# A two-block transformer kernel: in the experts, all low parts of the weights on VectorE, and the products that read them last in each piece

## The chip, the cores and the metric

The kernel runs on one core of one Trainium2 chip. The metric is the device time of one execution in microseconds (us). The time before is the median of three runs. One more execution was taken by the hardware profiler, and every row below is from that one.

Names of engines, as the profile has them: PE is TensorE (its matmuls), PEld is TensorE's loading of the stationary operand, DVE is VectorE, ACT is ScalarE, POOL is GpSimd, SP is SyncE, which here only issues DMAs.

## The reference, cut to what matters

The whole program is a first block (modulation, a mixer of attention and an mLSTM, then a mixture of experts) and a second block of two layers. The change is in the experts of the first block. Sixteen experts each choose 128 of 1024 tokens; a chosen token goes through two 1024x1024 products, a gate, and a third 1024x1024 product, and the result is added back to its row:

```python
def ec_moe(x, w_router, w_e_gate, w_e_up, w_e_down):
    ...
    g, idx = lax.top_k(aff.transpose(0, 2, 1), cap)
    xs = jax.vmap(lambda xb, ib: xb[ib])(x, idx)
    a = jnp.einsum('becd,edf->becf', xs, w_e_gate)
    u = jnp.einsum('becd,edf->becf', xs, w_e_up)
    y = jnp.einsum('becf,efd->becd', jax.nn.silu(a) * u, w_e_down) * g[..., None].astype(x.dtype)
```

All is float32. The three weights of an expert are 4 MB each.

## The kernel before

**A product in pieces.** `product(xT, w3)` multiplies 128 tokens by a 1024x1024 weight. It takes the weight in 8 pieces of 128 rows (`k`), and a DMA brings two pieces at a time (`ewr`, 10 buffers, or `ahead`, 2 buffers). The float32 operands are split into a high part (rounded to the matmul's type float32r) and a low part, the difference. For a piece, ScalarE makes the high part `ewH` of the raw weight (line 1183), and then the low part `ewL` is raw minus high: for six of the eight pieces on VectorE (line 1187), for the fourth and the eighth on GpSimd (line 1185). `ewH` and `ewL` have four buffers each, so the parts of a piece can be made once the matmuls of the piece four back have read theirs.

**Six matmuls a piece.** The tokens, turned, are split in the same way (`xTH`, `xTL`, or `eTH`, `eTL` for the third product). For each half of 512 columns `mm3` issues three matmuls, high times high (line 145), high tokens times low weights (line 146) and low tokens times high weights (line 147). So the second matmul of a piece already needs `ewL`.

**An expert.** In the order of the code: the products up(e), gate(e+1) and down(e), 24 pieces. Around them stand the smaller steps. `slots` makes eight tiles `hot` on VectorE (line 1198, 16 buffers), multiplies them on TensorE (line 1199) and copies the result to `idxT` and `gsl` on VectorE. `tokens` gathers the chosen rows `xs` by a DMA that GpSimd issues (line 1208). `transposed` turns 128x128 blocks on TensorE (line 1162) and splits them with ScalarE and VectorE (lines 141 and 142). VectorE multiplies up by the activated gate into `ea` (line 1232), and after down it scales the result into `ey` (line 1238), which GpSimd adds to the rows in memory by an indirect DMA (`acc_scr`, line 1239; called the scatter below).

**What sets the order.** Each engine works through its own queue in order. The queues' order is made when the kernel is built: a scheduler places each instruction by a simulated timeline. SP's queue holds the weight DMAs; each waits until both low parts of the pair that had its buffer have been made. `issue_after` and the number of buffers set what can run ahead.

Of the kernel before, what the change touches and what calls it, by code (L numbers as in the profile page):

```python
# [14 lines left out]
AF = mybir.ActivationFunctionType  # L15
OP = mybir.AluOpType
# [106 lines left out]
def build(ctx, tc, A, out):  # L123
# [6 lines left out]
    V, S, G, PE, SY = nc.vector, nc.scalar, nc.gpsimd, nc.tensor, nc.sync  # L130
# [4 lines left out]
    def load(pool, src, shape, name, eng=None, dt=F32, **kw):  # L135
        t = pool.tile(shape, dt, name=name, **kw)
        (eng or SY).dma_start(t, src)
        return t

    def split(H, L, src):  # L140
        S.activation(H, src, AF.Copy)  # L141
        V.tensor_sub(L, src, H)  # L142

    def mm3(o, lh, rh, start, stop):
        PE.matmul(o, lh[0], rh[0], start=start, stop=False)  # L145
        PE.matmul(o, lh[0], rh[1], start=False, stop=False)  # L146
        PE.matmul(o, lh[1], rh[0], start=False, stop=stop)  # L147
# [266 lines left out]
    with ExitStack() as es:  # L414
# [62 lines left out]
        for f2 in range(4):  # L477
            wt = wstream(wp, win, 704 + 256 * f2)
            for f in (2 * f2, 2 * f2 + 1):
# [5 lines left out]
                for t0, n in ((0, 256), (256, 512), (768, 512)):  # L485
                    more(late, 1)
                    pa = ps.tile([P, 512], F32, name="acc", bufs=4)
# [304 lines left out]
    with ExitStack() as es:  # L792
# [7 lines left out]
        op = att.enter_context(tile_pool(name="o", bufs=8, side="right", reuse_waits="tile"))  # L800
# [117 lines left out]
        for job in [(h, g, []) for h in range(8) for g in range(4)] + [None]:  # L918
            w = weights(*job) if job else iter(())
# [43 lines left out]
    with ExitStack() as es:  # L963
# [6 lines left out]
        with ExitStack() as es2:  # L970
# [6 lines left out]
            for k in range(8):  # L977
                t = load(sp, h_scr[k, :, C:N], [P, T], "hr")
                H = hp.tile([P, T], F32R, name=f"hH{k}")
                L = hp.tile([P, T], F32R, name=f"hL{k}")  # L980
                split(H, L, t)
                h.append((H, L))
            for f in range(8):
                rf = load(sp, r_scr[f], [P, T], "hr")
                sg = []
                for n0 in (Z0, GL0, GA0):
                    more(late, 1)
                    w = wstream(wp, win, n0 + P * f, P, bufs=(2, 4))
                    t = sp.tile([P, T], F32, name="sg", bufs=3)
                    for t0 in (0, 512):  # L990
                        sl = slice(t0, t0 + 512)
                        more(late, 1)
                        pa = ps.tile([P, 512], F32, name="acc", tag="acc", bufs=4)
# [58 lines left out]
        for i in range(8):  # L1052
# [3 lines left out]
            pa = outs[i] if i in outs else out_product((i,))[0]  # L1056
            for n in range(2):
                ns = slice(512 * n, 512 * n + 512)
# [45 lines left out]
    with ExitStack() as es:  # L1104
# [12 lines left out]
        pa = ps.tile([P, P], F32, name="pa")  # L1117
# [31 lines left out]
    with ExitStack() as es:  # L1149
        wp = es.enter_context(tile_pool(name="ew", bufs=1, reuse_waits="tile"))  # L1150
        tp = es.enter_context(tile_pool(name="et", bufs=2, side="right", reuse_waits="tile"))
        sp = es.enter_context(tile_pool(name="ex", bufs=2, reuse_waits="tile"))
        ps = es.enter_context(tile_pool(name="ps6", bufs=1, space=PSUM))
        g2B = load(sp, mod_scr[0, 3072:4096].partition_broadcast(P), [P, D], "g2B", bufs=1)

        def transposed(src, nm):
            H = tp.tile([P, 8, P], F32R, name=nm + "H")
            L = tp.tile([P, 8, P], F32R, name=nm + "L")
            for hb in range(2):
                pt = ps.tile([P, 512], F32, name="tp", tag="tp", bufs=2)  # L1160
                for j in range(4):
                    PE.transpose(pt[:, j * P:(j + 1) * P], src[:, (4 * hb + j) * P:(4 * hb + j + 1) * P], ident)
                hs_ = slice(4 * hb, 4 * hb + 4)
                split(H[:, hs_].rearrange("p a b -> p (a b)"), L[:, hs_].rearrange("p a b -> p (a b)"), pt)
            return H, L

        loads = [0]

        def product(xT, w3):
            pa = ps.tile([P, 2, 512], F32, name="acc", tag="acc", bufs=3)  # L1170
            for k2 in range(4):
                if ew_ahead:
                    raw = ew_ahead.pop(0)
                elif loads[0] % NB < AH:
                    raw = ahead(w3, k2)
                else:
                    raw = load(wp, pairs(w3, k2), [P, 2, D], "ewr", bufs=NB - AH)
                loads[0] += 1
                for kk in range(2):
                    k = 2 * k2 + kk  # L1180
                    H = wp.tile([P, D], F32R, name="ewH", bufs=4)
                    L = wp.tile([P, D], F32R, name="ewL", bufs=4)
                    S.activation(H, raw[:, kk], AF.Copy)  # L1183
                    if k % 4 == 3:
                        G.tensor_tensor(L, raw[:, kk], H, op=OP.subtract)  # L1185
                    else:
                        V.tensor_sub(L, raw[:, kk], H)  # L1187
                    for n in range(2):
                        ns = slice(512 * n, 512 * n + 512)
                        mm3(pa[:, n], (xT[0][:, k], xT[1][:, k]), (H[:, ns], L[:, ns]), k == 0, k == 7)  # L1190
            return pa.rearrange("p a b -> p (a b)")

        def slots(e):

            pi = ps.tile([P, 512], F32, name="tp", tag="tp", bufs=2)
            for i in range(8):
                hot = sp.tile([P, P], F32, name="hot", bufs=16)
                V.tensor_scalar(hot, ktop[:, P:2 * P], codeT[:, 16 * i + e:16 * i + e + 1], None, op0=OP.is_equal)
                PE.matmul(pi[:, 0:2], hot, pick[:, i, e, :], start=i == 0, stop=i == 7)
            ins = V.tensor_copy(idxT[:, e:e + 1], pi[:, 0:1])  # L1200
            V.tensor_copy(gsl[:, e:e + 1], pi[:, 1:2])
            return ins

        at = lambda e: bass.IndirectOffsetOnAxis(ap=idxT[:, e:e + 1], axis=0)

        def tokens(e):
            xs = sp.tile([P, D], F32, name="xs")
            G.indirect_dma_start(out=xs, out_offset=None, in_=h2_scr, in_offset=at(e))
            return xs

        def gated(xT, e):
            a = sp.tile([P, D], F32, name="ea")
            S.activation(a, product(xT, A["w_e_gate"][0, e]), AF.Silu)
            return a


        chosen = slots(0)
        xs = tokens(0)
        slots(1)
        xT = transposed(xs, "xT")  # L1220
        xs = tokens(1)
        with tc.issue_after(chosen.ins):
            a = gated(xT, 0)
        for e in range(16):
            more_ = e + 1 < 16
            if more_:
                xTn = transposed(xs, "xT")
            if e + 2 < 16:
                slots(e + 2)
                xs = tokens(e + 2)  # L1230
            pu = product(xT, A["w_e_up"][0, e])
            V.tensor_tensor(a, pu, a, op=OP.mult)
            if more_:
                an = gated(xTn, e + 1)
            hT = transposed(a, "eT")
            pd = product(hT, A["w_e_down"][0, e])
            y = sp.tile([P, D], F32, name="ey")
            V.scalar_tensor_tensor(y, pd, gsl[:, e:e + 1], g2B, op0=OP.mult, op1=OP.mult)
            G.indirect_dma_start(out=acc_scr, out_offset=at(e), in_=y, in_offset=None, compute_op=OP.add)
            if more_:  # L1240
                xT, a = xTn, an
# [495 lines left out]
```

## Time and profile before

| | us |
|---|---|
| three runs: median (lowest to highest) | 3382.16 (3378.16 to 3387.02) |
| the profiled execution: its own time | 3381.72 |
| span of its instructions in the profile | 3379.5 |
| first product of the experts starts, about | 1510 |
| scatter of expert 0, of expert 15 | 1567.4, 2148.5 |

The span is 2.2 us shorter than the execution's own time, and this does not change with what runs inside. The experts' products and their scatters lie between 1510 and 2148 us of the span. A row of the timeline gives the start, the duration, the engine, the line, the operation, the tiles, how many equal instructions are merged in the row, and in brackets how long the engine had been idle and what ended it. A matmul's duration is longer than the distance to the next one, because matmuls overlap; the distance between starts is its cost.

### The profile page before, as it was taken

The numbers are of one execution on the slowest core, as the hardware profiler recorded it, in microseconds if no ns is written. First come the engines' busy times: TensorE is split into PE (matmuls) and PEld (weight loads), VectorE is DVE, ScalarE is ACT, GpSimd is POOL, SyncE is SP. The second block draws the span as 40 slices with busy tenths as digits, with TensorE's granted clock in tenths as the row PEclk, the third lists the DMA queues.
The fourth block names the chain that finished last, engine by engine and source line by source line (L and its number), as shares of the span: only waits on it lengthen the run. The fifth ranks groups of instructions, "written<-read, shape, count | busy, mean of one in ns | idle before, by whom it ended". The sixth has DMA issues, their size and how long they took to land.

```text
span 3379.5 us, 48130 instructions
## 1 busy us (share of the span) xinstructions
PE 3158.9 (93%) x17297; PEld 2648.0 (78%) x17297; DVE 2259.6 (67%) x4772; ACT 1550.5 (46%) x3076; POOL 900.5 (27%) x936
## 2 busy tenths in 40 slices
PE   7997998999999999959999998799999898999999
PEld 5885877999998887848887777598876777887787
DVE  4485778667767563589999888777626745642773
ACT  4223453655555222217777666531126724312780
POOL 0012232222221000525555444320013601101450
PEclk9998999999999999969999999899999999999999
DMA  8531011000004341459999988433210033111002
GB/s 294 144 120 35 36 42 64 5 17 8 8 10 149 117 122 59 172 208 346 362 373 365 331 313 295 136 93 115 73 41 32 1 127 122 51 50 49 32 26 100
DMA packets 224011, 425.95 MB, mean 126 GB/s; under 512 B 28684, under 2 KB 121468, under 8 KB 223772
## 3 DMA queue, kind: packets, MB, share of 16 engines
q1 hardware_dynamic: 215708, 393.51, 33.3%
q0 software_dynamic: 8064, 29.36, 3.0%
q8 instruction: 136, 2.23, 0.3%
q14 instruction: 103, 0.84, 0.1%
HBM read 379.22 MB, written 43.61 MB: 125 GB/s over the span
## 4 chain that ended last, share of the span: by engine, by line
PE 67%; DVE 12%; issue 6%; DMA 4%; POOL 4%; ACT 4%; SPq 0%; ACTq 0%; POOLq 0%; DVEq 0%
PE acc L146 13%; PE acc L145 13%; PE acc L147 13%; DVE ewL L1187 2%; POOL ewL L1185 2%; PE s L145 2%; PE s L147 2%; PE s L146 2%; PE t L904 2%; PE o L1606 1%; PE u L763 1%; PE s L1564 1%; PE ni L744 1%; PE t L1590 1%; PE o L146 1%
## 5 line engine op out<-in xcount | busy, mean ns | idle before, releaser
L145 PE MATMUL acc<-hH,wHL 128*128 128x512 f32 (+1 forms) x1296 | 485.2, 376 | 4.7 <-ACT wHL L141 4.1
L146 PE MATMUL acc<-hL,wHL 128*128 128x512 f32 (+1 forms) x1296 | 484.3, 374 | 0.8 <-DVE hL L142 0.8
L147 PE MATMUL acc<-hH,wHL 128*128 128x512 f32 (+1 forms) x1296 | 482.5, 373 | 0.0
L1187 DVE TENSOR_TENSOR ewL<-ewr,ewH 128x1024 fp32r<-128x1024 f32 x240 | 388.7, 1658 | 54.4 <-ACT ewH L1183 54.1
L1183 ACT ACTIVATE ewH<-ewr 128x1024 fp32r<-128x1024 f32 x320 | 336.4, 1060 | 148.6 <-PE acc L147 143.8
L145 PEld LDWEIGHTS acc<-hH,wHL 128*128 128x128 f32 x1296 | 244.5, 189 | 52.7 <-ACT wHL L141 6.7
L146 PEld LDWEIGHTS acc<-hL,wHL 128*128 128x128 f32 x1296 | 244.6, 189 | 45.8 <-issue 2.6
L147 PEld LDWEIGHTS acc<-hH,wHL 128*128 128x128 f32 x1296 | 244.2, 189 | 44.2 <-issue 1.6
L1185 POOL TENSOR_TENSOR ewL<-ewr,ewH 128x1024 fp32r<-128x1024 f32 x80 | 219.0, 2738 | 198.9 <-ACT ewH L1183 198.7
L142 DVE TENSOR_TENSOR wHL<-wr,wHL 128x512 fp32r<-128x512 f32 (+1 forms) x160 | 111.7, 702 | 224.0 <-ACT wHL L141 223.4
L146 PE MATMUL acc<-ewL,xTH 128*128 128x512 f32 x512 | 208.6, 407 | 23.2 <-POOL ewL L1185 15.6
L142 DVE TENSOR_TENSOR et<-t,et 128x512 fp32r<-128x512 f32 x264 | 179.6, 685 | 64.0 <-ACT et L141 62.3
L141 ACT ACTIVATE et<-t 128x512 fp32r<-128x512 f32 x264 | 156.4, 605 | 134.0 <-PE t L904 111.8
L141 ACT ACTIVATE wHL<-wr 128x512 fp32r<-128x512 f32 (+1 forms) x160 | 101.9, 639 | 247.2 <-PE acc L146 222.1
L147 PE MATMUL acc<-ewH,xTL 128*128 128x512 f32 x512 | 203.4, 397 | 2.9 <-DVE xTL L142 2.9
L183 POOL TENSOR_SCALAR E<-E,sm 128x512 f32<-128x512 f32 (+1 forms) x192 | 117.5, 630 | 327.0 <-ACT E L172 107.0
L145 PE MATMUL acc<-ewH,xTH 128*128 128x512 f32 x512 | 203.2, 401 | 0.8 <-ACT xTH L141 0.8
L302 DVE SCALAR_TENSOR_TENSOR ga<-gw,lh,ga 128x512 f32<-128x512 f32 x224 | 161.0, 747 | 52.1 <-DMA gw<-in_w_mod_dram 51.0
L329 POOL TENSOR_TENSOR ga<-ga,gw 1x128 f32<-1x128 f32 (+1 forms) x48 | 42.4, 884 | 427.0 <-ACT ga L315 411.9
L170 DVE TENSOR_REDUCE sm<-s 128x1 f32<-128x512 f32 (+1 forms) x192 | 113.2, 597 | 60.2 <-PE s L888 53.3
L145 PE MATMUL acc<-wHL,hH 128*128 128x256 f32 (+1 forms) x464 | 142.8, 316 | 3.3 <-DVE hH L1283 2.1
L146 PEld LDWEIGHTS acc<-ewL,xTH 128*128 128x128 f32 x512 | 98.4, 192 | 56.5 <-POOL ewL L1185 22.5
(547 smaller groups left out, 8261.5 us busy)
## 6 DMA issues: line engine op xcount, KB each, us to landing
ewr<-in_w_e_up_dram SPq DMA_DIRECT2D x64, 1024.0 KB
ewr<-in_w_e_gate_dram SPq DMA_DIRECT2D x62, 1024.0 KB
wr<-in_w_in_dram SPq DMA_DIRECT2D x152, 256.0 KB
ewr<-in_w_e_down_dram SPq DMA_DIRECT2D x34, 1024.0 KB
ahead<-in_w_e_down_dram SPq DMA_DIRECT2D x30, 1024.0 KB
gw<-in_w_mod_dram SPq DMA_DIRECT2D x96, 256.0 KB
gw<-in_w_mod_dram SPq DMA_DIRECT2D x32, 512.0 KB
wm<-in_w_mod_dram SPq DMA_DIRECT2D x4, 2048.0 KB
```

Source lines behind the costliest of these rows:

```text
L141: S.activation(H, src, AF.Copy)
L142: V.tensor_sub(L, src, H)
L145: PE.matmul(o, lh[0], rh[0], start=start, stop=False)
L146: PE.matmul(o, lh[0], rh[1], start=False, stop=False)
L147: PE.matmul(o, lh[1], rh[0], start=False, stop=stop)
L170: V.tensor_reduce(ng[:, b:b + 1], sc, axis=AX.X, op=OP.max)
L183: G.tensor_scalar(E[:, k0:k0 + n], E[:, k0:k0 + n], f[:, b:b + 1], 1.0, op0=OP.mult, op1=OP.mult)
L302: V.scalar_tensor_tensor(acc[x], wk, ck, acc[x], op0=OP.mult, op1=OP.add) if k else
L904: PE.transpose(pt[:, kk * 256 + qi * P:kk * 256 + (qi + 1) * P], Es[qi][:, (2 * k2 + kk) * P:(2 * k2 + kk + 1) * P], ident)
L1183: S.activation(H, raw[:, kk], AF.Copy)
L1185: G.tensor_tensor(L, raw[:, kk], H, op=OP.subtract)
L1187: V.tensor_sub(L, raw[:, kk], H)
```

## The change

The low part is made by VectorE for all eight pieces (`split`, lines 140 to 142), so GpSimd makes none. The six matmuls of a piece come in another order: first the four that read the high part of the weight, for both halves of the columns, and then the two that read the low part. The number of matmuls and their operands are the same.

```diff
-                    S.activation(H, raw[:, kk], AF.Copy)
-                    if k % 4 == 3:
-                        G.tensor_tensor(L, raw[:, kk], H, op=OP.subtract)
-                    else:
-                        V.tensor_sub(L, raw[:, kk], H)
-                    for n in range(2):
-                        ns = slice(512 * n, 512 * n + 512)
-                        mm3(pa[:, n], (xT[0][:, k], xT[1][:, k]), (H[:, ns], L[:, ns]), k == 0, k == 7)
+                    split(H, L, raw[:, kk])
+
+                    for w, xs_ in ((H, xT), (L, xT[:1])):
+                        for n in range(2):
+                            for x in xs_:
+                                PE.matmul(pa[:, n], x[:, k], w[:, 512 * n:512 * n + 512], start=k == 0 and x is xT[0] and w is H,
+                                          stop=k == 7 and w is L)
```

The scheduler places the rest anew, so other instructions of the experts move too. Three places follow. Up to about the tenth expert the queues repeat from expert to expert; this is VectorE's queue in the middle of such an expert, from `ey` of the expert ahead to the low parts of the down product, before:

```order
L1238 SCALAR_TENSOR_TENSOR ey<-acc,gsl,g2B 128x1024
L1187 TENSOR_TENSOR ewL<-ewr,ewH 128x1024 x6
L1232 TENSOR_TENSOR ea<-acc,ea 128x1024
L1187 TENSOR_TENSOR ewL<-ewr,ewH 128x1024 x3
L142 TENSOR_TENSOR eTL<-tp,eTH 128x512 x2
L1187 TENSOR_TENSOR ewL<-ahead,ewH 128x1024 x3
L142 TENSOR_TENSOR xTL<-tp,xTH 128x512 x2
L1187 TENSOR_TENSOR ewL<-ewr,ewH 128x1024
```

and after (line numbers behind the change are lower by one, and `split` is line 142):

```order
L1197 TENSOR_SCALAR hot<-ktop,codeT 128x128
L142 TENSOR_TENSOR ewL<-ewr,ewH 128x1024 x8
L1231 TENSOR_TENSOR ea<-acc,ea 128x1024
L142 TENSOR_TENSOR ewL<-ewr,ewH 128x1024 x5
L142 TENSOR_TENSOR eTL<-tp,eTH 128x512 x2
L142 TENSOR_TENSOR ewL<-ahead,ewH 128x1024 x4
```

The low parts of all 24 pieces stand in this one queue now, with the other steps of VectorE between them. The same queue at the end of the expert, before:

```order
L1200 CAST idxT<-tp 128x1
L1201 COPY gsl<-tp 128x1
L1198 TENSOR_SCALAR hot<-ktop,codeT 128x128
L1187 TENSOR_TENSOR ewL<-ewr,ewH 128x1024 x3
L1238 SCALAR_TENSOR_TENSOR ey<-acc,gsl,g2B 128x1024
```

and after:

```order
L1197 TENSOR_SCALAR hot<-ktop,codeT 128x128 x4
L142 TENSOR_TENSOR ewL<-ewr,ewH 128x1024 x2
L1237 SCALAR_TENSOR_TENSOR ey<-acc,gsl,g2B 128x1024
L1197 TENSOR_SCALAR hot<-ktop,codeT 128x128 x2
L1199 CAST idxT<-tp 128x1
L1200 COPY gsl<-tp 128x1
```

`ey` moved ahead of `idxT`; three low parts of the next up product (pieces 0 to 2) stand ahead of it in both. The last place is TensorE's queue late in the stage, where the tokens of expert 12 are turned for its gate product (with buffer numbers; `acc_18551` is the up product of expert 11), before:

```order
L145 MATMUL acc_18551<-ewH_18586,xTH_18172 128x512
L1162 MATMUL tp_18508<-ident_68,xs_18215 128x128 x4
L1162 MATMUL tp_18515<-ident_68,xs_18215 128x128 x4
L146 MATMUL acc_18551<-ewL_18587,xTH_18172 128x512
L147 MATMUL acc_18551<-ewH_18586,xTL_18173 128x512
```

and after, without numbers:

```order
L1188 MATMUL acc<-ewL,xTH 128x512 x2
L1162 MATMUL tp<-ident,xs 128x128 x8
L1188 MATMUL acc<-ewH,xTH 128x512
L1198 MATMUL tp<-pick,hot 128x2 x8
L1188 MATMUL acc<-ewH,xTL 128x512
```

Before, the tokens are turned in the middle of the up product; now they are turned behind its last matmul, ahead of the gate product that reads them. Four of the later experts have it so, two of them two matmuls earlier. In the queues of the attention of layer 0, long behind the experts, rows change places too.

## Rows read from the trace of the kernel before

**Rows 1.** Stretches; busy us (count) of PE, PEld, DVE, ACT, POOL; clock, DMA share, GB/s.

```profile
1510.00:1567.40 57.40, 57.10 (x271) 46.71 (x269) 48.64 (x55) 43.13 (x46) 24.66 (x10) 0.97 0.74 279
1567.40:1865.00 297.60, 293.11 (x1401) 240.71 (x1402) 280.08 (x262) 224.13 (x232) 165.29 (x64) 1.00 0.99 366
1865.00:2117.10 252.10, 229.03 (x1018) 182.59 (x1018) 212.87 (x177) 165.34 (x171) 115.33 (x46) 0.97 0.87 307
2117.10:2148.50 31.40, 24.22 (x94) 17.97 (x92) 20.99 (x15) 13.88 (x16) 11.86 (x6) 0.89 0.23 60
```

**Rows 2.** Timeline of POOL: scatters of experts 0, 8, 14 and 15.

```profile
1567.40 2.42 POOL L1239 DMA_INDIRECT acc_scr<-ey,idxT  x1 [0.16 <-issue]
...
1864.79 2.37 POOL L1239 DMA_INDIRECT acc_scr<-ey,idxT  x1 [0.15 <-issue]
...
2117.10 2.29 POOL L1239 DMA_INDIRECT acc_scr<-ey,idxT  x1 [3.69 <-DVE ey L1238]
...
2148.46 1.75 POOL L1239 DMA_INDIRECT acc_scr<-ey,idxT  x1 [3.40 <-DVE ey L1238]
```

**Rows 3.** Timeline of PE in an early expert: products, transposes, the multiplied hot tiles.

```profile
1600.57 0.39 PE L145 MATMUL acc<-ewH,xTH 128*128 128x512 f32 x1
...
1603.98 0.39 PE L145 MATMUL acc<-ewH,xTH 128*128 128x512 f32 x1
...
1615.58 1.03 PE L1162 MATMUL tp<-ident,ea 128*128 128x128 f32 x8
1616.37 0.48 PE L146 MATMUL acc<-ewL,xTH 128*128 128x512 f32 x1
...
1628.04 1.39 PE L1199 MATMUL tp<-pick,hot 128*128 128x2 f32 x12
1629.30 0.49 PE L145 MATMUL acc<-ewH,eTH 128*128 128x512 f32 x1
```

**Rows 4.** PE's waits, 1567.4 to 1865 us: total us, times, longest.

```profile
PE acc L146 <- POOL ewL L1185: 3.6, 9, 1.3
```

**Rows 5.** The same, 1865 to 2117.1 us.

```profile
PE acc L146 <- POOL ewL L1185: 12.9, 13, 2.2
PE acc L146 <- DVE ewL L1187: 6.4, 10, 1.8
PE acc L147 <- DVE xTL L142: 2.9, 1, 2.9
```

**Rows 6.** Timeline of POOL and of PE where a late scatter is followed by a low part.

```profile
2032.53 2.32 POOL L1239 DMA_INDIRECT acc_scr<-ey,idxT  x1 [3.69 <-DVE ey L1238]
2034.30 2.93 POOL L1185 TENSOR_TENSOR ewL<-ewr,ewH 128x1024 fp32r<-128x1024 f32 x1
...
2037.28 0.50 PE L146 MATMUL acc<-ewL,xTH 128*128 128x512 f32 x1 [2.19 <-POOL ewL L1185]
```

**Rows 7.** Timeline of DVE: low parts alone, beside POOL's low part, beside POOL's DMA.

```profile
1631.17 1.06 DVE L1198 TENSOR_SCALAR hot<-ktop,codeT 128x128 f32<-128x128 f32 x5
...
1635.96 3.48 DVE L1187 TENSOR_TENSOR ewL<-ewr,ewH 128x1024 fp32r<-128x1024 f32 x3
...
2046.82 3.22 DVE L1187 TENSOR_TENSOR ewL<-ewr,ewH 128x1024 fp32r<-128x1024 f32 x1
...
2050.09 2.34 DVE L1187 TENSOR_TENSOR ewL<-ewr,ewH 128x1024 fp32r<-128x1024 f32 x2
```

**Rows 8.** Timeline of POOL at the last two places of Rows 7.

```profile
2046.57 2.39 POOL L1185 TENSOR_TENSOR ewL<-ewr,ewH 128x1024 fp32r<-128x1024 f32 x1 [4.22 <-ACT ewH L1183]
2050.38 1.81 POOL L1208 DMA_INDIRECT xs<-h_scr,idxT  x1 [1.42 <-DVE gsl L1201]
```

**Rows 9.** Groups, 1563.9 to 1712.8 us (four experts): busy us, mean ns | idle, releasers.

```profile
L1187 DVE TENSOR_TENSOR ewL<-ewr,ewH 128x1024 fp32r<-128x1024 f32 x61 | 91.4, 1538 | 8.0 <-ACT ewH L1183 8.0
L1183 ACT ACTIVATE ewH<-ewr 128x1024 fp32r<-128x1024 f32 x80 | 84.4, 1061 | 31.3 <-PE acc L147 30.2 <-DMA ewr<-in_w_e_up_dram 1.1
...
L142 DVE TENSOR_TENSOR eTL<-tp,eTH 128x512 fp32r<-128x512 f32 x8 | 5.1, 674 | 0.0
L1238 DVE SCALAR_TENSOR_TENSOR ey<-acc,gsl,g2B 128x1024 f32<-128x1024 f32 x4 | 5.1, 1271 | 0.0
L1232 DVE TENSOR_TENSOR ea<-acc,ea 128x1024 f32<-128x1024 f32 x4 | 4.8, 1210 | 0.0
```

**Rows 10.** Timeline of PE in the last expert.

```profile
2121.82 0.50 PE L146 MATMUL acc<-ewL,xTH 128*128 128x512 f32 x1 [2.16 <-POOL ewL L1185]
```

**Rows 11.** Busy time by engine in the attention of layer 0.

```profile
2560.00:2720.00 160.00, 142.46 (x974) 123.27 (x975) 126.01 (x367) 125.60 (x335) 86.63 (x120) 0.99 0.07 25
```

## The prediction

> **What bounds the kernel now.** I read the stretch of the experts by its parts first [rows 1]. The reader should see that PE is busy almost without a gap up to 1865 us (293 of 297.6 us) and less so behind it (229 of 252.1), and that no other engine is as full. The scatters, one for each expert, cut the stretch into periods [rows 2]: from expert 0 to 8 there are eight of (1864.79 - 1567.40) / 8 = 37.2 us, the early ones, and from 8 to 14 six of (2117.10 - 1864.79) / 6 = 42.05 us, the late ones. Behind expert 14 come 31.4 us for the last one.
>
> What PE must do for an expert comes from distances between starts [rows 3]. Fifteen product matmuls take 1603.98 - 1600.57 = 3.41 us, or 0.227 each, so a piece of six costs 1.364 us and 144 of them 32.7 us. Eight transposes take 0.79 us, so 16 take 1.6. Twelve records of the hot tiles take 1.26 us, so 16 take 1.7. The sum is 36.0 us. An early period is 1.2 us above that and a late one 6.05.
>
> The waits tell what the rest is. Early, PE waits almost only for GpSimd's low part [rows 4]. Late, the same wait is 12.9 us, VectorE's low part 6.4 and the turned tokens 2.9 [rows 5]. One late place shows the first of them whole [rows 6]: GpSimd sits 3.69 us until `ey` is there, issues the scatter (2.3 us), and only then makes its low part (2.9 us), for which PE has waited 2.19 us when it goes on.
>
> VectorE pays for GpSimd too [rows 7, 8]. Three low parts in a row take 3.48 us and two take 2.34, so one more costs 1.14 us. The one that started beside GpSimd's subtraction took 3.22 us. The two beside GpSimd's gather took their ordinary 2.34, so the DMAs that stay on GpSimd hold nobody up. Over four early experts a low part takes 1.54 us on the mean [rows 9].
>
> **The change part by part.** *Six low parts an expert leave GpSimd.* Its two indirect DMAs an expert stay. PE's waits for GpSimd's low part end, and VectorE's low parts fall from 1.54 to 1.14 us or, where one stands alone, to 2.34 - 1.14 = 1.20. *VectorE gets them.* For an expert it then has 24 low parts, 27.4 to 28.8 us; four halves of turned tokens at 0.674, 2.7; `ey` 1.27 and `ea` 1.21 [rows 9]; eight hot tiles at 1.06 / 5 [rows 7], 1.7; and about 0.1 for the two small copies. That is 34.4 to 35.8 us beside PE's 36.0. I take 34.4, since the low parts mostly stand in a row. So PE stays the bound, by little.
>
> Can a low part still be late? The worst regular place is the end of the down product. Three low parts of the next product are made there, and behind the last matmul stand `ey` (1.27), two hot tiles (0.4), the copies, which wait for the hot matmuls (about 0.5), and the fourth low part (1.2), with 0.16 for the last matmul's tail (0.39 less 0.23). That is 3.6 us. PE reads this low part after three pieces and four high matmuls, 3 x 1.364 + 0.9 = 5.0 us. The margin is 1.4 us. The new order of the six matmuls gives 0.7 of it (three more matmuls ahead of the first low one). ScalarE's high part takes 1.06 us [rows 9] and has nearly four pieces' time, so it isn't late.
>
> *Early periods.* All waits of PE go: 8 x (37.2 - 36.0) = 9.4 us less. If VectorE's queue holds PE at today's pace, it is nothing.
>
> *Late periods.* Without waits the six would take 216 us instead of 252.3. The new order puts a wait there. In four late experts the tokens are turned at the end of the up product, and VectorE has `ea` (1.21), a low part (1.14) and then the low half of the turned tokens (0.67) behind the product's tail (0.16): 3.2 us. PE has 0.8 us of transposes and one matmul meanwhile. The hot matmuls don't fill the rest, because their result takes one of the two buffers that the transposes hold until that half is made. So PE stands 2.2 us, or up to 2.9, the longest such wait now [rows 5]. Four times 2.6 is 10.4 us. The transposes of `ea` are cut into four or five groups in five experts, and a matmul behind such a group costs 0.1 us more (0.48 beside 0.39 [rows 3]): 2 us. After waits the granted clock falls: it is 0.97 late and 1.00 early [rows 1], which is 0.03 x 252 = 7.6 us between its two levels of 1.2 and 2.4 GHz. With fewer waits I take 4, between 0 and 7.6. Late: 216 + 10.4 + 2 + 4 = 232.4, which is 19.9 less.
>
> *Last expert.* It has one wait for GpSimd's low part, 2.16 us [rows 10], which goes. The turn of `ea` there is hidden by nothing, before or after.
>
> *Elsewhere.* The first expert may win up to 2 us; I take none. In the attention of layer 0 rows change places; PE is idle 17.5 of 160 us there [rows 11], and I take 0, between -5 and 5 by a third of that idle time.
>
> **The sum.** 9.4 + 19.9 + 2.2 = 31.5 us less. Against the profiled execution's 3381.7 that is 3350.2; the median of the runs lies 0.4 higher, which I leave out. The best end is all waits gone, 9.4 + 36.3 + 2.2 + 2 = 50 us less, 3332. The worst of this case has nothing early, and late 216 + 11.6 + 2 + 7.6 and today's 1.2 us in each period (7.2), 244.4, which is 7.9 less: with the last expert 10 us less, 3372.
>
> **The rivals.** *No wait is left late.* If VectorE runs ahead of the turned tokens, late periods are 36 us: 3332. For it speaks that the same steps cost nothing in early experts; against it, that the tokens are turned later than before in four experts.
>
> *Another engine keeps today's early pace.* VectorE would do so at 37.2 us with a few more waits, and the transfers could too: 366 GB/s are moved early at a DMA share of 0.99 [rows 1], that is 13.6 MB in 37.2 us, and 36.0 us would ask for 378. Then the early part gains nothing and the late one is 6 x 37.2 + 10.4 = 233.6, 18.7 less: with the last expert 3361. Against the transfers speaks that ScalarE waited for weights only 1.1 us in four experts [rows 9], and that twelve pairs are loaded ahead when the stage begins. The Trainium skill, page "Perfetto Trace Analysis", section "Roofline", gives 358 GB/s as a core's share of HBM, and about 120% of it as the practical ceiling of a core that is alone. By the first figure, as an estimate, a period could not be under 13.6 MB / 358 GB/s = 38.0 us and the early part would lose 6 us; the trace has held 366 for 297 us, so the share is no wall here, and the ceiling leaves room.
>
> *The late part keeps its length.* The waits for turned tokens and low clock take what GpSimd's waits give back: only the early part and the last expert gain, 11.6 us, 3370.
>
> *Slower: VectorE's single queue bounds.* It holds every low part now, behind steps that wait for PE. If `ey` costs it the 3.69 us that it costs GpSimd today [rows 6] and `ea` another 2.2, a period is 35.8 + 5.9 = 41.7 us, and fourteen are 584 beside today's 549.7: 34 us more, 3416. It decides from 39.3 us a period, that is, when the queue's waits pass 3.5 us an expert. For it speaks that 34.4 to 35.8 of 36.0 us are full; against it that three low parts are made when such a wait begins, 4.1 us of work for PE.
>
> **How the numbers follow.** My forecast has 0.45, no wait left 0.17, today's early pace 0.15, a late part as long as now 0.10, slower 0.13. The likeliest gives 3350. About 0.3%, 10 us, is what a measurement of this kernel can tell from no change, so the bounds are 3372 and 3392. Faster holds the first three and half of the fourth, 0.82; the same has the other half and a little of the last, 0.06; slower 0.12. The range from 3330 to 3372 takes in the first three and nearly all of the fourth; outside lie the slower case and a little on either side, under 0.2.
>
> **What would show it.** The profile after should have GpSimd with only indirect DMAs from 1510 us on, VectorE's low parts at 1.2 us, early periods between scatters of 36 us, late ones of 37 to 40, PE's longest waits there for the low half of the turned tokens, and no wait for transfers. Early periods of 37 us or more with VectorE busy without a gap would be the pace of another engine. Periods above 39.3 us with PE waiting for low parts would make the prediction wrong, and a gain above 50 us would mean that PE's work for an expert is less than 36.0 us.

## The result, and the profile after

The changed kernel takes 3338.9 us at the median of four runs (3336.3 to 3343.4), beside 3380.2 for the kernel before (3374.4 to 3387.0): a ratio of 0.9873, with an interval from 0.9857 to 0.9888. The profiled execution took 3336.3 us with a span of 3334.5, beside 3381.7 and 3379.5. So the span is 45.0 us shorter, and the median 41.3. The prediction said 31.5 less.

The scatters cut the span into the same parts as before. The second column is worked out from the rows of before, the third from those below.

| part of the span | before, us | after, us | difference | forecast |
|---|---|---|---|---|
| until the scatter of expert 0 | 1567.4 | 1560.7 | -6.7 | 0, up to -2 |
| eight early periods | 297.4 | 288.8 | -8.6 | -9.4 |
| six late periods | 252.3 | 234.0 | -18.3 | -19.9 |
| last expert | 31.4 | 24.8 | -6.6 | -2.2 |
| behind the last scatter | 1231.0 | 1226.2 | -4.8 | 0 (5 either way) |

The stretches of the changed kernel, with the columns of [rows 1]: start and end, its length, busy us (count) of PE, PEld, DVE, ACT and POOL, granted clock, DMA share, GB/s.

```profile
1510.00:1560.70 50.70, 50.70 (x251) 42.48 (x251) 45.52 (x56) 40.06 (x42) 5.37 (x2) 1.00 0.83 314
1560.70:1849.50 288.80, 288.80 (x1391) 242.18 (x1390) 272.85 (x313) 223.97 (x232) 52.32 (x17) 1.00 1.00 377
1849.50:2083.50 234.00, 225.03 (x1041) 184.77 (x1040) 203.78 (x215) 166.89 (x175) 24.15 (x12) 0.97 0.91 332
2083.50:2108.30 24.80, 20.94 (x93) 16.36 (x92) 18.95 (x18) 15.09 (x18) 2.35 (x2) 1.00 0.33 86
```

PE is busy in every microsecond of the first two stretches. GpSimd has only its DMAs left: 52.3 us of the early stretch, where it was 165.3 [rows 1]. The granted clock is 1.00 in three of the four stretches, where it was so in one. The scatters that bound these stretches, in the timeline of POOL (start, us; in brackets what POOL waited for):

```profile
1560.68 1.62 POOL L1238 DMA_INDIRECT acc_scr<-ey,idxT  x1 [28.00 <-DVE hot L1197]
...
1849.46 2.33 POOL L1238 DMA_INDIRECT acc_scr<-ey,idxT  x1 [23.73 <-DVE ey L1237]
...
2083.49 2.30 POOL L1238 DMA_INDIRECT acc_scr<-ey,idxT  x1 [36.94 <-DVE ey L1237]
2108.25 1.75 POOL L1238 DMA_INDIRECT acc_scr<-ey,idxT  x1 [22.45 <-DVE ey L1237]
```

An early period is 288.8 / 8 = 36.1 us. PE's waits between the scatters of experts 0 and 8, [rows 4] before, are none at all. Those between the scatters of 8 and 14, which answer to [rows 5], are all for turned tokens (us in total, times, longest):

```profile
PE tp L1198 <- DVE xTL L142: 5.6, 3, 2.3
PE acc L1188 <- DVE xTL L142: 2.3, 1, 2.3
PE acc L1188 <- ACT xTH L141: 1.1, 4, 0.3
```

The late periods are, in order, 35.5, 41.1, 40.6, 41.2, 36.4 and 39.3 us. The four long ones hold the four waits. One of the places, in the timelines of PE and of DVE:

```profile
1894.11 1.03 PE L1162 MATMUL tp<-ident,xs 128*128 128x128 f32 x8
1895.39 0.49 PE L1188 MATMUL acc<-ewH,xTH 128*128 128x512 f32 x1 [0.25 <-ACT xTH L141]
1897.32 1.95 PE L1198 MATMUL tp<-pick,hot 128*128 128x2 f32 x16 [1.43 <-DVE xTL L142]
...
1901.03 0.63 PE L1188 MATMUL acc<-ewH,xTH 128*128 128x512 f32 x1
...
1894.30 1.22 DVE L1231 TENSOR_TENSOR ea<-acc,ea 128x1024 f32<-128x1024 f32 x1 [1.65 <-PE acc L1188]
1895.44 1.22 DVE L142 TENSOR_TENSOR ewL<-ewr,ewH 128x1024 fp32r<-128x1024 f32 x1
1896.58 1.28 DVE L142 TENSOR_TENSOR xTL<-tp,xTH 128x512 fp32r<-128x512 f32 x2
```

PE turns the tokens and then stands, because VectorE first has `ea` and a low part to make, and the low half of the turned tokens comes last. Behind such a wait seven to nine matmuls run at the lower level of the clock: 0.63 us each, with 0.43 from one start to the next, where it is 0.39 and 0.227 otherwise [rows 3]. The granted clock, the last column but two, shows it behind the wait above:

```profile
1899.00:1903.00 4.00, 4.00 (x13) 3.18 (x13) 3.96 (x12) 1.08 (x2) 1.16 (x1) 0.57 1.00 372
```

VectorE's low parts, between 1610 and 1850 us (busy us, mean ns), where it was 1538 ns in [rows 9]:

```profile
L142 DVE TENSOR_TENSOR ewL<-ewr,ewH 128x1024 fp32r<-128x1024 f32 x132 | 155.7, 1220 | 10.1 <-ACT ewH L141 5.7 <-DMA ewr<-in_w_e_gate_dram 1.3 <-PE acc L1188 0.4
```

### The profile page after: what moved, and what is told of

Its sections match the earlier page's. It is cut to its first block, busy times and chain, and to the rows that moved or that the text cites. A ratio compares the mean times of both kernels' runs of the same rounds, so it can differ in the third digit from the quotient of the medians.

```text
span 3334.5 us, 48219 instructions
## 1 busy us (share of the span) xinstructions
PE 3142.5 (94%) x17297; PEld 2650.8 (79%) x17297; DVE 2239.7 (67%) x4868; ACT 1551.2 (47%) x3076; POOL 662.8 (20%) x840
## 5 line engine op out<-in xcount | busy, mean ns | idle before, releaser
L142 DVE TENSOR_TENSOR ewL<-ewr,ewH 128x1024 fp32r<-128x1024 f32 x320 | 377.9, 1220 | 37.1 <-ACT ewH L141 27.7
L1188 PE MATMUL acc<-ewL,xTH 128*128 128x512 f32 x512 | 162.5, 401 | 0.0
L145 PE MATMUL acc<-wHL,hH 128*128 128x256 f32 (+1 forms) x464 | 143.3, 317 | 3.3 <-DVE hH L1282 2.1
L146 PE MATMUL acc<-wHL,hH 128*128 128x256 f32 (+1 forms) x464 | 138.5, 304 | 0.0
L1564 DVE TENSOR_REDUCE mx<-s 128x1 f32<-128x512 f32 (+1 forms) x200 | 114.8, 588 | 28.3 <-PE s L1563 26.3
L147 PE MATMUL acc<-wHL,hL 128*128 128x256 f32 (+1 forms) x464 | 129.5, 314 | 4.4 <-DVE hL L1283 4.0
```

The costliest lines, as they stand in the source:

```text
L1188: PE.matmul(pa[:, n], x[:, k], w[:, 512 * n:512 * n + 512], start=k == 0 and x is xT[0] and w is H, stop=k == 7 and w is L)
L1564: V.tensor_reduce(mx[:, b:b + 1], sc[:, :n], axis=AX.X, op=OP.max)
```

## The experiments

After the result my theory was that GpSimd's low parts cost the time, in two ways that the prediction named: PE waits for them, because they stand behind a scatter in GpSimd's queue, and VectorE is slowed beside them. The rivals were the new order of the six matmuls, and the one place behind the scatter. All runs below are compared with the kernel before on the same chip. Code that no run touches also moves: the first matmuls of the `hot` tiles start at 1485.5 to 1496.5 us in the twelve programs, and behind the last scatter they take 1223.5 to 1237.0 us. So I read each run by its periods first. The periods are worked out from the scatters of each run as above.

| kernel | median, us | ratio (interval) | early period | late period |
|---|---|---|---|---|
| before | 3380 to 3384 | | 37.2 | 42.1 |
| changed | 3338.9 | 0.9873 (0.9857 to 0.9888) | 36.1 | 39.0 |
| order alone | 3385.0 | 1.0012 (0.9999 to 1.0025) | 39.6 | 40.7 |
| VectorE alone, old order | 3336.2 | 0.9868 (0.9851 to 0.9884) | 35.9 | 37.4 |
| GpSimd's low part unread | 3397.2 | 1.0054 (1.0036 to 1.0071) | 39.5 | 42.9 |
| GpSimd's low part left out | 3333.1 | 0.9863 (0.9847 to 0.9880) | 35.9 | 37.5 |
| the same, three slots | 3332.7 | 0.9861 (0.9840 to 0.9882) | 35.9 | 37.6 |
| GpSimd busy beside | 3398.1 | 1.0051 (1.0034 to 1.0068) | 39.9 | 42.8 |
| all but the place behind the scatter | 3368.8 | 0.9966 (0.9952 to 0.9980) | 37.3 | 40.7 |
| that place alone | 3363.9 | 0.9950 (0.9934 to 0.9967) | 35.7 | 41.5 |
| VectorE with 3.5 us more | 3338.7 | 0.9874 (0.9857 to 0.9890) | 37.4 | 36.5 |
| tokens turned earlier | 3326.4 | 0.9836 (0.9820 to 0.9853) | 36.1 | 36.0 |

**The two halves of the change.** The new order alone, in the kernel before:

```
-                    for n in range(2):
-                        ns = slice(512 * n, 512 * n + 512)
-                        mm3(pa[:, n], (xT[0][:, k], xT[1][:, k]), (H[:, ns], L[:, ns]), k == 0, k == 7)
+                    for w, xs_ in ((H, xT), (L, xT[:1])):
+                        for n in range(2):
+                            for x in xs_:
+                                PE.matmul(pa[:, n], x[:, k], w[:, 512 * n:512 * n + 512], start=k == 0 and x is xT[0] and w is H,
+                                          stop=k == 7 and w is L)
```

> The new order of the six matmuls alone; GpSimd keeps its six low parts an expert. If GpSimd's queue is the cause (my theory), the order gives each late low part 0.7 us: of the late waits for GpSimd (12.9 us, 13 of them) at most 9 us go, of those for VectorE (6.4 us, 10) most, early little (3.6 us), so some 10 to 15 us: 3365 to 3370, with waits for GpSimd's low part still seen late. If the order is what gives most, it lies near the changed kernel, 3340 to 3350, and early periods are 36.3 us.

Measured: 3385.0 us, no gain at all, with early periods of 39.6 us, 2.4 longer than before. An early place, in the timelines of POOL, DVE and PE:

```profile
1655.51 6.86 POOL L1242 DMA_INDIRECT acc_scr<-ey,idxT  x1 [0.49 <-DVE ey L1241]
1661.84 2.91 POOL L1185 TENSOR_TENSOR ewL<-ewr,ewH 128x1024 fp32r<-128x1024 f32 x1
...
1655.16 7.03 DVE L1187 TENSOR_TENSOR ewL<-ewr,ewH 128x1024 fp32r<-128x1024 f32 x6
...
1664.81 1.19 PE L1192 MATMUL acc<-ewL,xTH 128*128 128x512 f32 x4 [2.70 <-POOL ewL L1185]
```

Here the scatter begins 0.35 us behind the first of six low parts of VectorE in a row, and takes 6.86 us instead of 2.42 [rows 2]. GpSimd's own low part, behind it in the queue, starts that much later, and PE waits 2.70 us for it: the 0.7 us that the order gives is lost several times over. The four scatters that take 6 us and more are each followed by such a wait, 11.5 us in all. Both of my numbers for this run were wrong.

The other half, VectorE alone with the old order:

```
-                    S.activation(H, raw[:, kk], AF.Copy)
-                    if k % 4 == 3:
-                        G.tensor_tensor(L, raw[:, kk], H, op=OP.subtract)
-                    else:
-                        V.tensor_sub(L, raw[:, kk], H)
+                    split(H, L, raw[:, kk])
```

> VectorE alone makes the low parts, the six matmuls in the order of before. If GpSimd's queue is the cause, nearly all of the gain is here: 3339 to 3346, early periods 36.3 to 36.5 us, waits for VectorE's low part at most 1 us a late period. If the order matters most, the margin of 0.7 us at the end of the down product is too small: a wait for VectorE's low part in each period, early periods 37 us, 3360 or more.

Measured: 3336.2 us, the whole gain and the same as the changed kernel within the intervals. PE has no wait at all in early experts here either, so the margin of 0.7 us that is left without the new order was large enough. Late, PE waits for VectorE's low part in nine places, never for turned tokens, and the six periods take 224.7 us, 9.4 less than with the new order (us in total, times, longest):

```profile
PE acc L146 <- DVE ewL L142: 3.6, 9, 0.8
```

Beside VectorE's low parts the new order therefore brings nothing early and costs late, by way of the place at which the tokens come to be turned.

**The wait for GpSimd, or its work.** PE multiplies by an older low part where GpSimd makes one (in two of the eight pieces of each product, whose own low part is so left out), and GpSimd's result is read by nobody:

```
+                    low = prev if k % 4 == 3 else L
+                    prev = L
...
-                        mm3(pa[:, n], (xT[0][:, k], xT[1][:, k]), (H[:, ns], L[:, ns]), k == 0, k == 7)
+                        mm3(pa[:, n], (xT[0][:, k], xT[1][:, k]), (H[:, ns], low[:, ns]), k == 0, k == 7)
```

> The kernel before, but PE multiplies by the low part of the piece ahead where GpSimd makes one, so GpSimd's low part is made and read by nobody (products with the wrong low part of two pieces in eight). It takes the wait for GpSimd away and leaves GpSimd's work beside VectorE. If the wait is the cause: near the changed kernel, 3340 to 3350, with VectorE's low part still at 1.5 to 1.65 us on the mean. If GpSimd's slowing of VectorE is the cause: 3365 to 3380, with waits for VectorE's low part in place of GpSimd's.

Measured: 3397.2 us, slower than before. PE's waits for GpSimd are gone, and waits for VectorE's low part stand in their place. These waits from 1560 to 2117 us (total, times, longest), and an early place in the timelines of POOL and DVE:

```profile
PE acc L146 <- DVE ewL L1187: 25.5, 26, 2.1
```

```profile
1638.92 2.41 POOL L1185 TENSOR_TENSOR ewL<-ewr,ewH 128x1024 fp32r<-128x1024 f32 x1
1641.50 2.38 POOL L1241 DMA_INDIRECT acc_scr<-ey,idxT  x1 [0.17 <-issue]
1643.35 2.96 POOL L1185 TENSOR_TENSOR ewL<-ewr,ewH 128x1024 fp32r<-128x1024 f32 x1
...
1639.16 10.51 DVE L1187 TENSOR_TENSOR ewL<-ewr,ewH 128x1024 fp32r<-128x1024 f32 x5
```

Five low parts take 10.51 us where they would take 5 x 1.16 = 5.8; 4.7 are lost beside GpSimd's two. My theory's first half falls here: what PE waits for can be taken away and the time stays. But GpSimd still held the weights, the high part and a slot for a low part in this run, so it does not yet show that the slowing alone does it. Leaving GpSimd's low part out:

```
-                    L = wp.tile([P, D], F32R, name="ewL", bufs=4)
...
-                    if k % 4 == 3:
-                        G.tensor_tensor(L, raw[:, kk], H, op=OP.subtract)
-                    else:
+                    if k % 4 != 3:
+                        L = wp.tile([P, D], F32R, name="ewL", bufs=4)
```

> As before, but GpSimd's low parts are not made at all, and PE multiplies by the low part of the piece ahead there. VectorE has 18 low parts an expert and nothing beside it. If the wait is the cause it equals the run where nobody reads them, within 5 us; if the slowing of VectorE is, it is 15 to 30 us under that. Both theories give 3335 to 3345 here, since PE's work is the same; less than 3330 would mean that VectorE's 24 low parts still cost the changed kernel something.

Measured: 3333.1 us. Neither of my two pictures of it held as written, since the run where nobody reads is 64 us slower. But the early period, 35.9, is that of VectorE alone: the six low parts that VectorE takes over cost nothing early.

**GpSimd's arithmetic by itself.** To the run with the low parts left out, work was added whose result nobody reads. It subtracts `g2B`, a constant that `ey` reads too, from itself:

```
+        def beside(ins):
+            with tc.issue_after(ins.ins):
+                for _ in range(3):
+                    G.tensor_tensor(junk, g2B, g2B, op=OP.subtract)
```

It is called behind the gather and behind the scatter. Room for `junk` came from the slots of `ewL`, three instead of four, for which there is a control.

> As the run in which GpSimd's six low parts are left out, but GpSimd subtracts a constant tile from itself six times an expert, three times behind each of its two DMAs: nothing reads these, they read nothing that VectorE or PE use, and nobody waits for them (VectorE has three slots for its low parts, as room was needed). If GpSimd's arithmetic costs by slowing VectorE alone: VectorE's low parts are 1.4 us or more on the mean, PE waits for them at the end of the down product, early periods 37 us or more, 3355 to 3400. If the cost needs GpSimd's place in PE's chain (its result, or a buffer that it holds), it equals the run with three slots and no such work, within 5 us.

> The run in which GpSimd's low parts are left out, with three slots for VectorE's low parts in place of four: the control of the run beside it. If three slots are enough for VectorE's 18 low parts, 3333 as with four; if they cost something, that is the part of the other run that isn't GpSimd's arithmetic.

Measured: 3398.1 us with the work beside, 3332.7 in the control. Between 1610 and 1850 us, the largest group of VectorE's low parts, with the work and then without it (busy us, mean ns):

```profile
L1185 DVE TENSOR_TENSOR ewL<-ewr,ewH 128x1024 fp32r<-128x1024 f32 x90 | 162.6, 1842 | 12.1 <-ACT ewH L1182 7.9 <-PE acc L146 2.5
```

```profile
L1185 DVE TENSOR_TENSOR ewL<-ewr,ewH 128x1024 fp32r<-128x1024 f32 x99 | 120.2, 1224 | 31.1 <-ACT ewH L1182 21.8 <-PE acc L146 5.1 <-DMA ewr<-in_w_e_up_dram 0.7
```

An early place of the run with the work, in the timelines of POOL, DVE and PE:

```profile
1689.58 16.66 POOL L1209 TENSOR_TENSOR junk<-g2B 128x1024 f32<-128x1024 f32 x6
...
1690.23 11.41 DVE L1185 TENSOR_TENSOR ewL<-ewr,ewH 128x1024 fp32r<-128x1024 f32 x4 [0.23 <-PE acc L146]
...
1698.87 0.50 PE L146 MATMUL acc<-ewL,xTH 128*128 128x512 f32 x1 [1.16 <-DVE ewL L1185]
1701.70 0.50 PE L146 MATMUL acc<-ewL,xTH 128*128 128x512 f32 x1 [1.16 <-DVE ewL L1185]
```

Each low part takes 2.85 us there, as long as one GpSimd subtraction (16.66 / 6 = 2.78): the two engines go in turn. No engine waits for GpSimd's work, it holds no buffer of the others, and yet the kernel loses 65 us. So GpSimd's arithmetic costs by slowing VectorE, and that suffices. How much it costs depends on where it stands: all six came in a row behind the scatter in this run, worse than in the kernel before. Whether GpSimd's place in PE's chain would cost anything without the slowing was not tried, because its subtraction can't be had without it here.

**One place, or all of them.** The low part behind the scatter (the fourth of the up product) was taken from GpSimd, or left to it alone:

```
-                    if k % 4 == 3:
+                    if k % 4 == 3 and not (k == 3 and loads[0] % 12 == 6):
```

> The kernel before, but the fourth low part of the up product, the one that stands behind the scatter in GpSimd's queue, is VectorE's; GpSimd keeps the five others of an expert. If the loss sits in that one place (GpSimd's scatter, then its low part, beside VectorE's own run of low parts there), nearly all of the gain comes: early periods 36.3 to 36.6 us, 3338 to 3346. If each low part on GpSimd costs its share by slowing VectorE, a sixth of 44 us comes: some 3373.

```
-                    if k % 4 == 3:
+                    if k == 3 and loads[0] % 12 == 6:
```

> GpSimd makes that one low part of an expert alone, VectorE the 23 others, in the order of matmuls of before. If the loss sits in that place, it stays: early periods of 37 us or more, 3365 to 3385. If it goes by the number of GpSimd's low parts, a sixth of it stays: some 3343.

Measured: 3368.8 and 3363.9 us. The early periods speak against the place: 37.3 us with the five others, as long as before, and 35.7 with that one alone. The reason is in the timelines of DVE and POOL of the second run: GpSimd's low part comes ahead of the scatter there, beside `ey`, which it doesn't slow (1.28 us, [rows 9] 1.27), and only the three low parts behind lose a little, 4.73 us instead of 3.48 [rows 7].

```profile
1743.79 1.28 DVE L1238 SCALAR_TENSOR_TENSOR ey<-acc,gsl,g2B 128x1024 f32<-128x1024 f32 x1
1745.37 4.73 DVE L1187 TENSOR_TENSOR ewL<-ewr,ewH 128x1024 fp32r<-128x1024 f32 x3 [0.30 <-ACT ewH L1183]
...
1744.34 2.41 POOL L1185 TENSOR_TENSOR ewL<-ewr,ewH 128x1024 fp32r<-128x1024 f32 x1 [3.57 <-issue]
```

The Trainium skill, page "SBUF — State Buffer", section "Who interferes with whom", says that a VectorE instruction with two inputs in SBUF contends with a GpSimd instruction that reads SBUF, for a pair of ports that it calls an exclusive lock, while one with at most one such input, outside the modes that take both ports, does not. The trace agrees on both: a low part (`ewr` and `ewH`) begun 0.25 us behind GpSimd's ended 1.08 us behind the end of it [rows 7, 8], and `ey`, whose large operands are `acc` in PSUM and `g2B`, kept its length. The `hot` tiles, which read one large tile (`codeT`), were held up too: they took 424 ns on the mean before and 278 after, between 1510 and 2150 us, and the first expert below shows one place of it.

The late periods of the second run are another matter, 41.5 us. An example from its timelines of DVE and PE:

```profile
1933.34 1.28 DVE L1238 SCALAR_TENSOR_TENSOR ey<-acc,gsl,g2B 128x1024 f32<-128x1024 f32 x1 [2.88 <-PE acc L147]
...
1935.82 0.50 PE L146 MATMUL acc<-ewL,xTH 128*128 128x512 f32 x1 [2.29 <-DVE ewL L1187]
1940.76 0.51 PE L146 MATMUL acc<-ewL,xTH 128*128 128x512 f32 x1 [0.33 <-DVE ewL L1187]
```

The longer of the two waits is not GpSimd's: VectorE sat 2.88 us in front of `ey` with a low part queued behind it that PE needed next. That is the prediction's slower rival at one place, in a program in which the order of VectorE's queue came out that way. So these two runs are no clean test of the place, and the share of a single low part stays open.

**VectorE's room.** In the changed kernel the sixth low part of each product is made twice:

```
                     split(H, L, raw[:, kk])
+                    if k == 5:
+                        V.tensor_sub(L, raw[:, kk], H)
```

> The changed kernel, in which VectorE makes the sixth low part of every product twice: 3 x 1.15 = 3.5 us more an expert, with the same output. If VectorE's load is 34.4 of 36.3 us as counted, it becomes 37.9 and sets the pace: early periods of 37.9 us or a little more, fifteen of which are 24 us or more, 3363 to 3384. If VectorE had more room than that, the time stays at 3339.

Measured: 3338.7 us, no slower, although VectorE does set the pace. From 1610 to 1850 us, the busy times and PE's wait:

```profile
1610.00:1850.00 240.00, 235.83 (x1135) 195.17 (x1134) 239.20 (x274) 180.85 (x189) 75.41 (x13) 1.00 1.00 364
```

```profile
PE acc L1190 <- DVE ewL L1185: 4.2, 6, 0.8
```

VectorE is busy 239.2 of 240 us and a period is 37.4, so its load without the three is 37.4 x 0.997 - 3 x 1.15 = 33.8 us, beside the 34.4 counted. The changed kernel's own early stretch gives 272.85 / 8 = 34.1. The early part loses 10 us, as it should. The total doesn't show it, because the late periods came down from 39.0 to 36.5: in this program the tokens are turned early in the late experts too, and no wait for them is left. In the profiled executions the losses (10.1 us early, 2.8 in the last expert, 1.9 in the first and 4.2 in code ahead of the experts and behind them) stand against a gain of 14.9 late, which leaves 4.1; the medians are 0.2 apart.

**The turned tokens.** The second half of the up product is queued behind the turning of the next tokens (`xlast` keeps their last transpose):

```
                 xTn = transposed(xs, "xT")
+                last = xlast[0]
...
+                    if after and k == 4:
+                        tc_hold = tc.issue_after(after.ins)
+                        tc_hold.__enter__()
...
-            pu = product(xT, A["w_e_up"][0, e])
+            pu = product(xT, A["w_e_up"][0, e], last if more_ else None)
```

> The changed kernel, in which the matmuls of the second half of the up product are queued behind the turning of the next tokens, so that these aren't turned at the product's end in late experts. If the turn just in time is what makes four late periods 39 to 41 us, all late periods come down to 36.3 to 37 and PE has no wait for the turned tokens: 14 to 18 us less than the changed kernel, 3320 to 3326, give or take 5 us for the attention behind. If the late periods are long for another reason (clock, weights at the stage's end), it stays at 3335 to 3340.

Measured: 3326.4 us, 12.5 below the changed kernel and the fastest of all. Between the scatters of experts 8 and 14 PE waits for nothing:

```profile
1855.70:2071.70 216.00, 216.00 (x1041) 180.86 (x1041) 202.18 (x215) 168.18 (x175) 26.47 (x11) 1.00 0.96 360
```

Six periods in 216.0 us are the 6 x 36.0 that the prediction gave for late experts without waits, and the clock is 1.00. The theory of the turned tokens holds: turned elsewhere, they give back 18.0 us late, half of it waits and half PE's busy time (225.0 to 216.0). The total shows less, since the code ahead of the experts, which the edit doesn't touch, ends 6.2 us later in this program. With the old order and VectorE alone the same periods lose 8.7 us, 4.1 of it in waits, nearly all for low parts.

## Why the prediction was right, point by point

*PE bounds, at 36.0 us an expert.* Right. Early periods are 36.1 us without a wait, and 36.0 late once nothing stands in the way.

*Early periods, 9.4 us.* 8.6 came. The part about the cause is only half right. The prediction let PE's wait for GpSimd go, and named the slowing of VectorE as a second price. The runs show the second as the cause that suffices: without the wait the time was no shorter, and with the slowing alone it was as long. Nor could the gain be read from the waits that the trace lists, 3.6 us [rows 4]: of the 8.8 us between the two early stretches, 4.5 were PE's idle time and 4.3 its busy time (293.11 to 288.80).

*Late periods, 19.9 us.* 18.3 came. The four places were the four foreseen. PE stands 7.9 us there for the low halves and 1.1 for the high ones, where 10.4 were forecast, and its busy time is 225.0 us, 9.0 above the 216, where 6 were taken for the lower clock and the cut transposes. The prediction put this wait down to the new order, and two runs agree: VectorE alone has none, and the order alone has it (10.9 us from expert 8 to 14). But two programs with the old order have it too, 8.0 us with GpSimd's low part unread and 11.0 with GpSimd busy beside. So what decides is where the scheduler puts the turning; the order of the six matmuls is one of the things that move it.

*The new order gives 0.7 us of a margin of 1.4.* The size may be right (the terms on VectorE's side add up to 3.5 us, not 3.6, which makes the margin 1.5), but nothing needed it. VectorE alone gives the gain without the order, and the order alone gives nothing.

*VectorE's load, 34.4 to 35.8 us.* Just under its lower end: 34.1 in the changed kernel, 33.8 by the run that overloaded it.

*The first expert, 0, up to 2 us.* Mis-sized: 6.7, of which 0.2 lie ahead of the experts. PE waited 11.03 us for the first gather of tokens and then 8.40, which is 2.6. The gather waits for `gsl`, and ahead of that VectorE makes `hot` tiles; before, a low part of GpSimd lay beside them. The timelines of DVE and POOL before, and of DVE after:

```profile
1490.18 6.76 DVE L1198 TENSOR_SCALAR hot<-ktop,codeT 128x128 f32<-128x128 f32 x23
1493.91 2.36 POOL L1185 TENSOR_TENSOR ewL<-ahead,ewH 128x1024 fp32r<-128x1024 f32 x1 [29.80 <-ACT ewH L1183]
...
1489.94 4.59 DVE L1197 TENSOR_SCALAR hot<-ktop,codeT 128x128 f32<-128x128 f32 x23
```

The rest is the first product itself: PE starts it at 1510.4 us before and at 1507.5 after, and the scatter follows 57.0 and 53.2 us later, with a clock of 0.97 [rows 1] and 1.00. The prediction moved the low parts off GpSimd without looking at what the first of them lay beside.

*The last expert, 2.2 us.* Mis-sized: 6.6. The wait for GpSimd went [rows 10]. No lower clock had followed that wait: the granted clock was 1.00 from 2122 to 2128 us. The clock fell at the turn of `ea`, which the prediction took as the same before and after. Before, VectorE's low part beside GpSimd's (2129.92 to 2132.27 us) took 3.20 us there, so that the low half `eTL` came late and PE waited 1.20 us for it. The lower clock lay around that wait, from 2131.6 to 2138.4 us. The timelines of DVE and PE, and the stretch:

```profile
2130.15 3.20 DVE L1187 TENSOR_TENSOR ewL<-ewr,ewH 128x1024 fp32r<-128x1024 f32 x1
...
2134.01 0.80 PE L147 MATMUL acc<-ewH,eTL 128*128 128x512 f32 x1 [1.20 <-DVE eTL L142]
...
2132.00:2136.00 4.00, 2.80 (x7) 1.70 (x7) 2.55 (x3) 0.06 (x1) 0.27 (x1) 0.50 0.00 0
```

After, that wait is 0.23 us and the clock stays at 1.00. Why it fell before and not after, behind a wait of 1.6 us for `ea` in one and 1.73 in the other, is not shown. PE's busy time for the same work is 20.94 us instead of 24.22 [rows 1], which is 3.3 of the 6.6; the other 3.3 are idle time. The prediction counted one wait of GpSimd's doing and set the turn at nothing. What is left of waiting is the turn of `ea`, which it called uncovered:

```profile
2093.59 1.09 PE L1162 MATMUL tp<-ident,ea 128*128 128x128 f32 x8 [1.73 <-DVE ea L1231]
```

*The attention behind, 0.* It took 4.8 us less, within the 5 given. Twelve programs with the same code there lie between 1223.5 and 1237.0 us, so this belongs to no step of the change.

*The rivals.* The early pace of another engine: the transfers now run at 377 GB/s at a share of 1.00 and PE doesn't wait for them, so they did not hold 37.2 us. VectorE's queue as the bound: not in the changed kernel, and at 37.4 us a period in the run that adds 3.5 us. The late part as long as now: no. No wait left late: not in the changed kernel, but the run with tokens turned earlier is that case.

In short, the sum came out 13.5 us too small: the first expert, the last one and the attention behind gave 15.9 us more than forecast, and the experts between them 2.4 less. So the median of 3338.9 us lies 11 below the forecast of 3350. The experts between were right in size, with a part of the gain put down to the wait and to the new order, which the runs don't bear out.

## What to carry to other kernels

Before work is shared between VectorE and GpSimd, look in the trace at how long VectorE's instruction takes beside GpSimd's and how long alone: if the two go in turn, as here, GpSimd's share is paid twice, and VectorE may do all of it in no more time than its part of it took. Here VectorE was busy 280.08 / 8 = 35.0 us an early period with three quarters of the low parts [rows 1], and 34.1 with all of them. A wait that the profile names is not yet the cause: take away the wait and leave the work, and then leave the work and take away every link to it. And where a scheduler orders the program anew, read a run by stretches, since a gain and a loss of 10 us can hide in one total.

## What the runs showed of the hardware that I had not expected

VectorE's low parts hold up an indirect DMA of GpSimd that begins when they are already under way. The scatter took 2.42 us in the kernel before [rows 2], 6.86 where it began 0.35 us behind the first of six in a row, and 9.14 in the run where VectorE is busy without a break:

```profile
1677.70 9.14 POOL L1240 DMA_INDIRECT acc_scr<-ey,idxT  x1 [0.63 <-DVE ey L1239]
```

A row of low parts that begins behind the DMA does not do this. In the changed kernel an early scatter begins 0.35 us ahead of eight low parts:

```profile
1633.28 1.59 POOL L1238 DMA_INDIRECT acc_scr<-ey,idxT  x1 [29.35 <-DVE hot L1197]
...
1633.63 9.77 DVE L142 TENSOR_TENSOR ewL<-ewr,ewH 128x1024 fp32r<-128x1024 f32 x8
```

The gather shows the same. Begun inside a row of low parts it takes 5.02 us in the changed kernel, where it took 1.81 before [rows 8]:

```profile
1562.60 5.02 POOL L1207 DMA_INDIRECT xs<-h_scr,idxT  x1 [0.30 <-DVE ewL L142]
```

In the run with GpSimd's low parts left out it begins 0.32 us ahead of a low part in early experts and takes 0.97. How much is lost inside a row is not settled: a gather begun 0.1 us behind the first of three low parts took 1.97 us in the kernel before and 4.24 in the run with GpSimd's low part unread.

The prediction had read from two low parts beside a gather that the DMAs hold nobody up, which is right: the six beside the scatter of 6.86 us took 7.03, or 1.17 each. It did not ask the other way round. In the run with scatters of 9.14 us PE waits for neither GpSimd nor a gather. Where a low part of GpSimd that PE needs stands behind the DMA in GpSimd's queue, as with the order alone, PE waits for it.
